# Loads of K, Q and V for two groups at a time, over one shared block of ones

## The chip, the cores and the metric

The kernel runs on one core of one Trainium2 chip. The time is the device time of the program in microseconds (us), taken from several runs; a profiled run gives the span and the trace, which begin a little later and end a little earlier than the timed run (before: 127.74 us timed, 126.0 us span). Ratios are the mean time of one kernel's fast runs over that of the other's fast runs of the same rounds, with a 95% interval; so they are not quite the ratio of the medians that stand beside them.

The engines are called PE (TensorE matmul), DVE (VectorE), ACT (ScalarE), POOL (GpSimd) and SP (SyncE).

## The reference

Linear attention on 8 x 12 heads, 512 positions, 64 dimensions, in fp32:

```python
Q_feat = np.maximum(0, Q) + 1
K_feat = np.maximum(0, K) + 1
KV = np.einsum('bhkd,bhkv->bhdv', K_feat, V)
K_sum = np.sum(K_feat, axis=2)
numerator = np.einsum('bhqd,bhdv->bhqv', Q_feat, KV)
denominator = np.einsum('bhqd,bhd->bhq', Q_feat, K_sum)
return numerator / (denominator[:, :, :, None] + 1e-10)
```

Q, K, V and the output are 12.58 MB each: 37.75 MB to read and 12.58 MB to write, with little arithmetic per byte.

## The kernel before

The work is cut into 12 groups of 8 heads. Each group needs K and Q on 128 partitions, and V as four blocks: block b holds V on partitions 32b to 32b+31 and zeros elsewhere; a fifth block holds ones in four columns, from which the matmul gets the sum of K. POOL issues the loads, which cast fp32 to bf16 (K of group 0 alone comes through SP, in fp32); it also issues most stores. Three V buffers, each with its own zeros and its own block of ones, go round. The code is cut, and the comments are added.

```python
NV = 3
v_blk = [const.tile([P, 5, 2, C2, D], BF16, name=f"v_blk{i}") for i in range(NV)]
...
def load_k(g):      # one DMA: 1.05 MB read, half of it written
    ...
def load_v(g):
    for b in range(4):
        nc.gpsimd.dma_start(
            out=v_blk[g % NV][32 * b : 32 * b + 32, b],
            in_=v_dram[32 * b : 32 * b + 32, 2 * g : 2 * g + 2],
        )
...
# the start: K and Q of groups 0 and 1 are issued, then
nc.vector.memset(flat[0][:, 0:part], 0.0)       # first clear, DVE's part; ACT has the rest
...
load_v(0)
nc.vector.memset(flat[1][:, 0:part], 0.0)       # second clear
...
make_identity(nc, identity)
for t in kva_diag:
    nc.gpsimd.memset(t, 0.0)
load_v(1)
load_k(2)
k_features(0)
q_features(0)
nc.vector.memset(flat[2][:, 0:part], 0.0)       # third clear
...
load_v(2)
load_q(2)
for g in range(NG - 1):
    if g:
        k_features(g); q_features(g); transposes(g - 1)
    if g >= 2:
        output(g - 2)
    keys_values(g)
    if g + AHEAD < NG:                          # AHEAD = 3
        load_k(g + AHEAD); load_v(g + AHEAD); load_q(g + AHEAD)
    if g >= LAG:
        store(g - LAG)
```

## Time and profile before

| | before |
|---|---|
| time, median (range) | 127.88 us (127.55 to 127.98) |
| span of the profiled run | 126.0 us |
| PE, DVE, ACT, POOL busy | 55%, 53%, 37%, 42% of the span |
| DMA, each of the 38 middle slices | 90% or more |
| transfers issued | 86 |

The row to read first is the DMA row: no engine that computes is busy much more than half of the time, and the DMA engines never rest. The prediction below shows these lines and works with them. The count of packets: 1376 small ones are the completions of 86 transfers on 16 engines.

```profile
DMA packets 14186, 32.13 MB, mean 255 GB/s; under 512 B 1376, under 2 KB 1376, under 8 KB 14176
```

### The profile page before, as it was taken

Reading aid. Unit: us, or ns where it says so; the run is one execution under the profiler, and the core shown is the slowest. Engines: PE = TensorE matmul, PEld = TensorE weight load, DVE = VectorE, ACT = ScalarE, POOL = GpSimd, SP = SyncE. Lnnn points to the kernel's source line nnn. Section 1 sums busy time; section 2 is a strip of 40 time slices with the busy share of each in tenths; the row PEclk is TensorE's granted clock in tenths of the full one; section 3 lists DMA queues with packets and bytes.
Section 4 is the critical chain, followed back from the end, with each engine's and each line's share of the span. In section 5 each row is a group of like instructions: output and inputs, shape, how many; then the busy total and the mean of one; then the engine's idle time right before and its main releaser. Section 6 shows DMA issues by size and latency. Waiting matters only on the chain.

```text
span 126.0 us, 2374 instructions
## 1 busy us (share of the span) xinstructions
PE 69.4 (55%) x960; PEld 51.1 (41%) x960; DVE 66.3 (53%) x155; ACT 47.1 (37%) x76; POOL 53.4 (42%) x91
## 2 busy tenths in 40 slices
PE   0000099719859089682971980890693496966100
PEld 0000087507647067462750660670562365744100
DVE  4898802077193582938607605723921944769400
ACT  7950007930645505554073054036019009290000
POOL 6695785616346156452372274263353341200000
PEclk9999999995999976999599589679869959996555
DMA  3999999999999999999999999999999999999993
GB/s 82 337 208 213 204 208 208 212 212 208 211 206 213 207 208 213 206 298 293 200 252 336 198 213 370 213 209 360 228 208 321 267 206 284 425 410 418 413 403 121
DMA packets 14186, 32.13 MB, mean 255 GB/s; under 512 B 1376, under 2 KB 1376, under 8 KB 14176
## 3 DMA queue, kind: packets, MB, share of 16 engines
q0 software_dynamic: 12816, 28.84, 98.8%
q1 hardware_dynamic: 1360, 3.15, 6.7%
q8 instruction: 7, 0.11, 0.3%
q14 instruction: 3, 0.02, 0.0%
HBM read 37.75 MB, written 12.58 MB: 400 GB/s over the span
## 4 chain that ended last, share of the span: by engine, by line
DMA 67%; DVE 9%; PE 8%; POOL 6%; issue 4%; POOLq 0%
DMA k_raw<-in_K_dram 25%; DMA q_raw<-in_Q_dram 17%; DMA v_blk<-in_V_dram 16%; DMA out_dram<-o_sb 9%; DVE o_sb L184 7%; PE kva_ps L141 5%; POOL v_blk L93 4%; POOL q_raw L100 2%; PE qt_ps L160 2%; DVE recip L183 1%; PE o_ps L173 1%; DVE qf L116 1%; POOL k_raw L86 1%; POOL zero L195 0%; POOLq L100 0%
## 5 line engine op out<-in xcount | busy, mean ns | idle before, releaser
L141 PE MATMUL kva_ps<-v_blk,kf 128*64 128x320 bf16 x384 | 40.6, 385 | 15.8 <-DMA v_blk<-in_V_dram 15.8
L141 PEld LDWEIGHTS <-kf 128*64 128x64 bf16 x384 | 27.9, 143 | 24.8 <-DVE qf L116 15.8
L93 POOL DMA_DIRECT2D v_blk<-in_V_dram x48 | 26.3, 552 | 27.0 <-DMA k_raw<-in_K_dram 14.8
L173 PE MATMUL o_ps<-kva_diag,qt 128*64 128x130 bf16 x384 | 19.1, 234 | 32.0 <-DVE o_sb L184 31.3
L184 DVE TENSOR_TENSOR o_sb<-o_ps,recip 128x512 f32<-128x512 f32 x48 | 33.2, 691 | 1.6
L151 ACT CAST kva_diag<-kva_ps 64x256 bf16<-64x256 f32 x24 | 8.9, 372 | 65.2 <-PE kva_ps L141 64.9
L161 ACT COPY qt<-qt_ps 128x1024 bf16<-128x1024 bf16 x24 | 29.5, 1301 | 0.3
L173 PEld LDWEIGHTS <-qt 128*64 128x64 bf16 x384 | 12.7, 114 | 37.5 <-DVE o_sb L184 35.8
L116 DVE TENSOR_SCALAR qf<-q_raw 128x1024 bf16<-128x1024 bf16 x24 | 9.2, 424 | 32.9 <-DMA q_raw<-in_Q_dram 32.9
L116 DVE TENSOR_SCALAR kf<-k_raw 128x1024 bf16<-128x1024 bf16 (+1 forms) x24 | 10.9, 497 | 10.3 <-DMA k_raw<-in_K_dram 10.3
L107 POOL DMA_DIRECT2D out_dram<-o_sb x10 | 7.7, 774 | 16.1 <-DMA q_raw<-in_Q_dram 7.8
L160 PE MATMUL qt_ps<-identity,qf 128*128 128x128 bf16 x192 | 13.1, 223 | 0.0
L160 PEld LDWEIGHTS <-qf 128*128 128x128 bf16 x192 | 11.1, 99 | 3.4 <-issue 3.2
L183 DVE RECIPROCAL recip<-o_ps 128x8 f32<-128x8 f32 x48 | 9.5, 198 | 4.1 <-PE o_ps L173 4.1
L86 POOL DMA_DIRECT2D k_raw<-in_K_dram x11 | 7.8, 713 | 8.4 <-DMA out_dram<-o_sb 3.7
L100 POOL DMA_DIRECT2D q_raw<-in_Q_dram x12 | 8.8, 730 | 4.4 <-DMA v_blk<-in_V_dram 2.5
L152 ACT CAST kva_diag<-kva_ps 64x4 bf16<-64x4 f32 x24 | 4.0, 168 | 0.0
L206 DVE MEMSET v_blk<- 128x2925 f32 x1 | 2.5, 2496 | 0.7 <-DVE ones L202 0.7
L224 DVE MEMSET v_blk<- 128x2925 f32 x1 | 2.5, 2496 | 0.6 <-issue 0.6
L212 DVE MEMSET v_blk<- 128x2925 f32 x1 | 2.5, 2496 | 0.6 <-issue 0.6
L219 POOL MEMSET kva_diag<- 128x520 bf16 x3 | 2.0, 720 | 0.0
L207 ACT COPY v_blk<-zero 128x2195 f32<-128x2195 f32 x1 | 2.0, 2020 | 0.0
(15 smaller groups left out, 7.9 us busy)
## 6 DMA issues: line engine op xcount, KB each, us to landing
out_dram<-o_sb POOLq DMA_DIRECT2D x10, 1024.0 KB, 12.1
q_raw<-in_Q_dram POOLq DMA_DIRECT2D x12, 512.0 KB, 11.1
v_blk<-in_V_dram POOLq DMA_DIRECT2D x48, 128.0 KB, 9.5
k_raw<-in_K_dram POOLq DMA_DIRECT2D x11, 512.0 KB, 12.0
out_dram<-o_sb SPq DMA_DIRECT2D x4, 512.0 KB, 7.6
k_raw<-in_K_dram SPq DMA_DIRECT2D x1, 1024.0 KB, 5.0
```

What stands on the lines that cost most here:

```text
L86: (nc.sync if g == 0 else nc.gpsimd).dma_start(out=k_raw, in_=k_dram[:, g * 2 : g * 2 + 2])
L93: nc.gpsimd.dma_start(out=v_blk[g % NV][32 * b : 32 * b + 32, b], in_=v_dram[32 * b : 32 * b + 32, 2 * g : 2 * g + 2],)
L100: nc.gpsimd.dma_start(out=q_raw, in_=q_dram[:, g * 2 : g * 2 + 2])
L107: nc.gpsimd.dma_start(out=o_to, in_=o_sb)
L116: nc.vector.tensor_scalar(out=dst, in0=src, scalar1=1.0, scalar2=1.0, op0=ALU.add, op1=ALU.max)
L141: nc.tensor.matmul(kva_ps[64 * n : 64 * n + 64], lhsT=kf[:, c, n, :], rhs=vb[:, :, n, c, :], start=(c == 0), stop=(c == C2 - 1),)
L151: nc.scalar.copy(out=kva[ps, :, n, 0:D], in_=kva_ps[ps, 0:4, :])
L160: nc.tensor.transpose(qt_ps[:, c, :], qf[:, half * C + c, :, :], identity)
L161: nc.scalar.copy(out=qt[:, :, :, half], in_=qt_ps)
L173: nc.tensor.matmul(ops[c // 4][64 * j : 64 * j + 64, c // 2 % 2, (c % 2) * W : (c % 2) * W + W], lhsT=qt[:, c, 32 * b : 32 * b + 32, :], r ...
L183: nc.vector.reciprocal(out=recip, in_=cells[:, :, :, :, D:D1])
L184: nc.vector.tensor_tensor(out=o_sb[:, h:NP:2, 4 * i : 4 * i + 4].rearrange("p n (b c) d -> p b c n d", b=2), in0=cells[:, :, :, :, 0:D], i ...
```

## The change

The intent is to have fewer and larger transfers: in the middle of the run K and Q of two groups come with one DMA each and V of two groups with four, and the loads stay two pairs ahead. Two V buffers, each for a pair of groups, are laid into one tile of nine blocks, 0 to 3 and 5 to 8, and share the ones in block 4; `own(g)` picks a group's half of its pair's buffer. The first two groups and the last two are still loaded one at a time. The core of the diff, cut, with one comment added:

```diff
-    v_blk = [const.tile([P, 5, 2, C2, D], BF16, name=f"v_blk{i}") for i in range(NV)]
+    v_all = const.tile([P, 9, 4, C2, D], BF16, name="v_all")
+    v_blk = [v_all[:, 5 * i : 5 * i + 4] for i in range(2)]
...
+    def own(g):
+        return slice(g % 2 * 2, g % 2 * 2 + 2)
...
+    def load(s):
+        pair = (2 * s, 2 * s + 1)
+        for groups in ((pair,) if s < NG // 2 - 1 else ((pair[0],), (pair[1],))):
+            load_k(s, groups)
+            load_v(s, groups)
+            load_q(s, groups)
...
+    def clear(blocks, ms, parts):       # DVE zeroes blocks up to parts, ACT the rest
...
-        nc.vector.memset(flat[0][:, 0:part], 0.0)
...
-        load_v(0)
-        nc.vector.memset(flat[1][:, 0:part], 0.0)
...
+        clear((0, 5), own(0), 3)
+        mark(own(0))
+        load_v(0, (0,))
+        clear((0, 5), own(1), 3)
+        mark(own(1))
         make_identity(nc, identity)
         for t in kva_diag:
             nc.gpsimd.memset(t, 0.0)
-        load_v(1)
-        load_k(2)
+        load_v(0, (1,))
+        load_k(1, (2, 3))
         k_features(0)
         q_features(0)
...
+        clear((5, 9), slice(0, 4), 7)
+        load_v(1, (2, 3))
+        load_q(1, (2, 3))
...
-            if g + AHEAD < NG:
-                load_k(g + AHEAD)
-                load_v(g + AHEAD)
-                load_q(g + AHEAD)
+            if g % 2 and g // 2 + 2 < NG // 2:
+                load(g // 2 + 2)
```

More of the change, by code (lines that the diff above doesn't have):

```diff
@@ L13 @@
 BANK = 512
-IN_BUFS = 4
+IN_BUFS = 2
 OUT_BUFS = 6
 LAG = 3
-AHEAD = 3
 @with_exitstack
@@ L73 @@
     kva_diag = [const.tile([P, 4, 2, D1], BF16, name=f"kva_diag{i}") for i in range(NV)]
+    k_bufs = {}
+    q_bufs = {}
     k_in = {}
@@ L80, with load_k, load_v, load_q @@
     outs = {}
-    def load_k(g):
-        k_raw = (head_pool if g == 0 else in_pool).tile(
-            [P, 2, C2, D], FP32 if g == 0 else BF16, name="k_raw"
-        )
-        (nc.sync if g == 0 else nc.gpsimd).dma_start(
-            out=k_raw, in_=k_dram[:, g * 2 : g * 2 + 2]
-        )
-        k_in[g] = k_raw
-    def load_v(g):
+    def own(g):
+        return slice(g % 2 * 2, g % 2 * 2 + 2)
+    def load_k(s, groups):
+        if groups == (0,):
+            k_raw = head_pool.tile([P, 2, C2, D], FP32, name="k_first")
+            nc.sync.dma_start(out=k_raw, in_=k_dram[:, 0:2])
+            k_in[0] = k_raw
+            return
+        if s not in k_bufs:
+            k_bufs[s] = in_pool.tile([P, 4, C2, D], BF16, name="k_raw")
+        ms = slice(groups[0] % 2 * 2, groups[-1] % 2 * 2 + 2)
+        nc.gpsimd.dma_start(
+            out=k_bufs[s][:, ms], in_=k_dram[:, 2 * groups[0] : 2 * groups[-1] + 2]
+        )
+        for g in groups:
+            k_in[g] = k_bufs[s][:, own(g)]
+    def load_v(s, groups):
+        ms = slice(groups[0] % 2 * 2, groups[-1] % 2 * 2 + 2)
         for b in range(4):
             nc.gpsimd.dma_start(
-                out=v_blk[g % NV][32 * b : 32 * b + 32, b],
-                in_=v_dram[32 * b : 32 * b + 32, 2 * g : 2 * g + 2],
-            )
-    def load_q(g):
-        q_raw = in_pool.tile([P, 2, C2, D], BF16, name="q_raw")
-        nc.gpsimd.dma_start(out=q_raw, in_=q_dram[:, g * 2 : g * 2 + 2])
-        q_in[g] = q_raw
+                out=v_blk[s % 2][32 * b : 32 * b + 32, b, ms],
+                in_=v_dram[32 * b : 32 * b + 32, 2 * groups[0] : 2 * groups[-1] + 2],
+            )
+    def load_q(s, groups):
+        if s not in q_bufs:
+            q_bufs[s] = in_pool.tile([P, 4, C2, D], BF16, name="q_raw")
+        ms = slice(groups[0] % 2 * 2, groups[-1] % 2 * 2 + 2)
+        nc.gpsimd.dma_start(
+            out=q_bufs[s][:, ms], in_=q_dram[:, 2 * groups[0] : 2 * groups[-1] + 2]
+        )
+        for g in groups:
+            q_in[g] = q_bufs[s][:, own(g)]
+    def load(s):
[4 more added lines that the diff above has]
+            load_q(s, groups)
     def store(g):
@@ L110, in store @@
             nc.sync.dma_start(out=o_to[:, h:NP:2], in_=o_sb[:, h:NP:2])
-    def edge(i):
-        return v_blk[i][:, 4, :, :, 0:4].rearrange("p n c j -> p (n c) j")
     def feature(dst, src):
@@ L136, in keys_values @@
         kf = kfs.pop(g)
-        vb = v_blk[g % NV]
+        sb = g // 2 % 2
+        vb = v_all[:, 4 * sb : 4 * sb + 5, own(g)]
         kva_ps = psum_kva.tile([P, 5, D], FP32, name="kva_ps")
@@ L150, in keys_values @@
             ps = slice(64 * n, 64 * n + 64)
-            nc.scalar.copy(out=kva[ps, :, n, 0:D], in_=kva_ps[ps, 0:4, :])
-            nc.scalar.copy(out=kva[ps, :, n, D], in_=kva_ps[ps, 4, 0:4])
+            nc.scalar.copy(out=kva[ps, :, n, 0:D], in_=kva_ps[ps, sb : sb + 4, :])
+            nc.scalar.copy(out=kva[ps, :, n, D], in_=kva_ps[ps, 4 - 4 * sb, 0:4])
     def transposes(g):
@@ L192, in output, with mark @@
         outs[g] = o_sb
+    def clear(blocks, ms, parts):
+        for eng, bs in zip((nc.vector, nc.scalar), (slice(blocks[0], parts), slice(parts, blocks[1]))):
+            t = v_all[:, bs, ms].rearrange("p b m c d -> p b (m c d)").bitcast(FP32)
+            if eng is nc.vector:
+                eng.memset(t, 0.0)
+            else:
+                eng.copy(out=t, in_=zero[:, :, None].to_broadcast([P, t.shape[1], t.shape[2]]))
+    def mark(ms):
+        e = v_all[:, 4, ms, :, 0:4].rearrange("p m c j -> p (m c) j")
+        nc.vector.tensor_copy(out=e, in_=ones[:, None, :].to_broadcast([P, e.shape[1], 4]))
     with tc.manual_schedule():
         nc.gpsimd.memset(zero, 0.0)
-        load_k(0)
-        load_q(0)
-        load_k(1)
-        load_q(1)
+        for g in range(2):
+            load_k(0, (g,))
+            load_q(0, (g,))
         nc.vector.memset(ones, 0.0)
@@ L202 @@
             nc.vector.memset(ones[32 * b : 32 * b + 32, b : b + 1], 1.0)
-        flat = [t.rearrange("p b n c d -> p (b n c d)").bitcast(FP32) for t in v_blk]
-        width = flat[0].shape[1]
-        part = width * 4 // 7
-        nc.vector.memset(flat[0][:, 0:part], 0.0)
-        nc.scalar.copy(
-            out=flat[0][:, part:width], in_=zero.to_broadcast([P, width - part])
-        )
-        nc.vector.tensor_copy(out=edge(0), in_=ones[:, None, :].to_broadcast([P, 2 * C2, 4]))
-        load_v(0)
-        nc.vector.memset(flat[1][:, 0:part], 0.0)
-        nc.scalar.copy(
-            out=flat[1][:, part:width], in_=zero.to_broadcast([P, width - part])
-        )
-        nc.vector.tensor_copy(out=edge(1), in_=ones[:, None, :].to_broadcast([P, 2 * C2, 4]))
+        clear((0, 5), own(0), 3)
[3 more added lines that the diff above has]
+        mark(own(1))
         make_identity(nc, identity)
@@ L219 @@
             nc.gpsimd.memset(t, 0.0)
-        load_v(1)
-        load_k(2)
+        load_v(0, (1,))
+        load_k(1, (2, 3))
         k_features(0)
         q_features(0)
-        nc.vector.memset(flat[2][:, 0:part], 0.0)
-        nc.scalar.copy(
-            out=flat[2][:, part:width], in_=zero.to_broadcast([P, width - part])
-        )
-        nc.vector.tensor_copy(out=edge(2), in_=ones[:, None, :].to_broadcast([P, 2 * C2, 4]))
-        load_v(2)
-        load_q(2)
+        clear((5, 9), slice(0, 4), 7)
+        load_v(1, (2, 3))
+        load_q(1, (2, 3))
         for g in range(NG - 1):
```

## The prediction

> **What bounds the kernel now.** I read the page's DMA rows first, then the chain of waits, then the busy table by stretch, then the timelines of the first 16 us and of one steady period.
>
> ```profile
> DMA  3999999999999999999999999999999999999993
> GB/s 82 337 208 213 204 208 208 212 212 208 211 206 213 207 208 213 206 298 293 200 252 336 198 213 370 213 209 360 228 208 321 267 206 284 425 410 418 413 403 121
> ...
> HBM read 37.75 MB, written 12.58 MB: 400 GB/s over the span
> ...
> DMA 67%; DVE 9%; PE 8%; POOL 6%; issue 4%; POOLq 0%
> ```
>
> The DMA engines are 90% busy or more in every slice between the first and the last, while PE is busy 55%, DVE 53%, POOL 42% and ACT 37% of the span. The GB/s row counts what is written: a load that casts fp32 to bf16 reads twice what it writes, so 208 to 213 there is 416 to 426 of reading, and the stores of the last slices move 403 to 425. Both kinds of traffic therefore run at about 419 GB/s of HBM bytes. All bytes are 37.75 + 12.58 = 50.33 MB; at 419 that is 120.1 us of the 126.0 us span. The rest is the start, the end, and small change. So: any moment in which the DMA queues are empty is added to the time, and faster engines gain nothing.
>
> The busy table by stretch (columns: stretch, its length, busy us of PE, PEld, DVE, ACT, POOL, granted clock, DMA share, GB/s) shows that they are empty only at the two ends:
>
> ```profile
> 0.00:2.00 2.00, 0.00 (x0) 0.00 (x0) 0.33 (x6) 1.26 (x1) 0.99 (x6) 1.00 0.10 18
> ...
> 10.00:15.00 5.00, 0.00 (x0) 0.00 (x0) 4.44 (x8) 0.00 (x0) 2.82 (x6) 1.00 1.12 209
> 15.00:20.00 5.00, 4.22 (x44) 3.40 (x45) 0.16 (x1) 0.44 (x3) 3.75 (x7) 1.00 1.11 207
> ...
> 124.00:126.00 2.00, 0.00 (x0) 0.00 (x0) 0.00 (x0) 0.00 (x0) 0.00 (x0) 0.50 0.06 25
> ```
>
> A steady period of the POOL timeline, whose transfers all go through one queue, gives the durations:
>
> ```profile
> 80.12 0.70 POOL L86 DMA_DIRECT2D k_raw<-in_K_dram  x1 [1.78 <-DMA out_dram<-o_sb]
> 82.57 2.18 POOL L93 DMA_DIRECT2D v_blk<-in_V_dram  x4 [1.76 <-DMA k_raw<-in_K_dram]
> 85.70 0.72 POOL L100 DMA_DIRECT2D q_raw<-in_Q_dram  x1 [0.95 <-DMA v_blk<-in_V_dram]
> 87.65 0.79 POOL L107 DMA_DIRECT2D out_dram<-o_sb  x1 [1.23 <-DMA q_raw<-in_Q_dram]
> 90.16 0.70 POOL L86 DMA_DIRECT2D k_raw<-in_K_dram  x1 [1.72 <-DVE recip L183]
> ```
>
> POOL waits before each issue for the landing of an earlier transfer of the same kind: in the built order each waits for the semaphore that the eighth transfer before it used (DMASW0 to 7 go round), so at most eight are in flight. The releases are thus landing times: store to K 2.45 us, K to Q 5.08 (four V and one Q), Q to store 2.51. A MB costs 2.5 us whatever its kind, and POOL's waits here cost nothing: about 10 us of transfers lie ahead in the queue.
>
> **What the Trainium skill says.** The Trainium skill, "DMA: Bandwidth & Descriptors", section "Bandwidth", advises to batch to 1 MiB and more for 75% of peak; that would speak for the change, whose K and Q loads double from 1 to 2 MB read and V pieces from 256 to 512 KB. The trace does not bear it out for a queue that stays full: with the small pieces it moves 419 GB/s already, against the 435 which the same section gives as the fabric's ceiling. The section "Anatomy of one DMA — SWDGE (gpsimd) path" puts about 2.0 us of fixed setup and completion on each transfer, most of it the wait for the last byte's confirmation, and says that DMA engines do not wait on semaphores, the issuing sequencer does. Back to back this overlaps, as the trace shows; where an issue must wait for a landing with nothing else queued it is paid. The section "Why a DMA increments its semaphore by 16 and not by 1" has each of 16 engines end a transfer with a small semaphore write. The page agrees: 1376 packets are under 512 B, and 10+12+48+11+4+1 = 86 issues times 16 is 1376.
>
> **The change part by part.**
>
> *Fewer, larger transfers.* K goes from 12 to 8 issues, Q from 12 to 8, V from 48 to 32; stores stay at 14. That is 86 to 62, or 24 x 16 = 384 small packets less. Bytes are the same. What one completion costs: over three periods V and Q together took 4.96, 5.02 and 5.08 us between releases (the last is shown above), mean 5.02; two K-sized transfers take 2 x 2.42 (2.39 and 2.45 seen). The 0.18 left is for three more completions: 0.06 each. 24 x 0.06 = 1.4 us at most; I take 0.8, since a V piece also differs in writing 32 partitions only. POOL saves some 24 issues of 0.54 to 0.73 us, off the path.
>
> *Depth of prefetch.* Two groups per slot, two slots. V for the next pair waits for the second group of the old pair. By hand, with 5 us for each pair transfer and 2.5 per store: after the V of a pair has landed, Q, K, V, Q, the next K and two to four stores (25 to 35 us) lie before the V that reuses its slot; Q's landing (5 us) and two compute iterations of about 6.5 us put that issue at about 18 us. The queue stays fed. At the tail POOL issues six stores after the last load instead of five; the last Q comes 2.5 us earlier and the sum of bytes is as before. Nothing lost, nothing won.
>
> *The first clears.* Here I see the cost. The timeline of before's start:
>
> ```profile
> 5.06 2.50 DVE L212 MEMSET v_blk<- 128x2925 f32 x1 [0.55 <-issue]
> ...
> 9.40 1.36 POOL L93 DMA_DIRECT2D v_blk<-in_V_dram  x2
> 11.17 0.54 POOL L93 DMA_DIRECT2D v_blk<-in_V_dram  x1 [0.41 <-issue]
> ...
> 13.44 0.75 POOL L93 DMA_DIRECT2D v_blk<-in_V_dram  x1 [1.74 <-DMA q_raw<-in_Q_dram]
> ...
> 14.18 0.72 POOL L86 DMA_DIRECT2D k_raw<-in_K_dram  x1
> ...
> 15.78 3.66 PE L141 MATMUL kva_ps<-v_blk,kf 128*64 128x320 bf16 x32 [15.78 <-DMA v_blk<-in_V_dram]
> ```
>
> The second clear runs at 5.06, so V of group 1 is issued from 9.40 and follows V of group 0 without a gap. In the changed kernel groups 0 and 1 share one tile, and the built order has a wait that was not there:
>
> ```
> DVE  L222 Memset v_all 128x3x1024 [waits DMASW5_49,DMASW4_49]
> POOL L107 DMACopy v_all<-in_V_dram 32x2x1024 [waits DVE_49]
> ```
>
> Those two semaphores, each at its first count, are the second and third V transfers of group 0. No byte overlaps: the clear is for group 1's part of blocks 0 to 2. But the stretch from its first to its last address takes in group 0's part of blocks 1 and 2, which is exactly what is waited for (blocks 0 and 3 are not). So the second clear begins when the third V piece has landed, and POOL, which runs in order, can issue V of group 1 and all that follows only after it. By then the queue has drained.
>
> Sizes: Q of group 1 landed at 13.16 (the POOL row at 13.44 and the chain), V pieces of 0.63 us follow: the third at 13.16 + 3 x 0.63 = 15.05, the fourth at 15.7 (PE starts at 15.78). The clear has 3072 columns: 2.50 x 3072/2925 = 2.62 us, to 17.7. From landing to landing the skill's fixed cost is about 2.0; the fourth piece still moves 0.63 us meanwhile. Empty queue: 2.0 - 0.63 + 2.62 + 0.1 to 0.6 for semaphores and issue = 4.1 to 4.6, taken as 4.4.
>
> *After it.* DVE then has the mark of ones, the features of K (2.48) and Q (0.74) of group 0 and a clear of 4096 columns (3.50), about 7.4 with gaps: to about 25.2, when V of groups 2 and 3 may go. V of group 1 and the K pair (2.5 + 5) feed the queue from about 19.3 to 26.8; first data of V about 1.5 us after 25.2. Just covered; I add 0.3.
>
> Sum: +4.4 +0.3 -0.8 = +3.9; 127.88 + 3.9 = 131.8 us.
>
> **Rivals.** (1) The wait is hidden and only the packets count: 127.88 - 0.8 = 127.1, at best 126.5. For it: landings of other transfers hide POOL's waits all through the middle. Against it: at 15 us nothing else can be queued, since POOL stands at the wait. (2) The middle starves as well, because V of a pair waits for two groups' matmuls, which are slowed to 4.01 us each where the clock is granted at 0.83 or less: one bubble of 1 us per pair in four pairs, 136. Against it: the 7 us and more of slack above. (3) Larger transfers move at a better rate: 425 in place of 419 GB/s would take 1.7 us off, to 130.1. For it: 425 stands in one slice of stores; against it: stores of 1 MB and V pieces of 128 KB written run alike.
>
> **Range and chances.** The bubble can be 3.5 to 5.2, the second gap 0 to 1, the saving 0 to 1.8: 130.2 to 133.2 should hold it 8 times in 10. Slower by over 2% begins at 130.44, so it is likely: 0.87. Within 2% (a short bubble with a large saving): 0.12. Faster by over 2% would need 125.3, less than the bytes allow with any gap: 0.01.
>
> **What would show it.** In the busy table the stretch 15 to 19 us should have a DMA share far under 0.5, where before it was 1.11. In the timeline the second DVE clear should start at about 15.1 instead of 5.06, released by a V landing, and V of group 1 be issued at about 17.8. DMA packets under 512 B should be 62 x 16 = 992. From 27 us to the end the DMA row should be full again and the spacing of releases 5 us per pair transfer. I am wrong if the second clear starts before 10 us, if the DMA row has gaps past 30 us, or if the released spacing is shorter than 4.9 us per 2 MB by more than the completions explain.

## The result, and the profile after

The changed kernel took 135.63 us (median of four runs, 134.18 to 136.11) beside 127.90 for the kernel before: ratio 1.0591, interval 1.0503 to 1.0679. Executions over 1.5% slower than the fastest of the same kernel are left out of the means. It is slower, as forecast, but by 7.7 us and not by 3.9; 135.63 lies outside the range of 130.2 to 133.2.

The page of the changed kernel has these rows in place of those quoted of before:

```profile
DMA  4999509899999999999999999999999999999991
GB/s 110 312 211 210 95 0 132 137 200 211 210 210 214 209 210 212 212 212 208 211 240 407 298 189 209 209 229 405 313 208 209 210 227 393 422 419 411 402 389 57
DMA packets 13803, 32.12 MB, mean 239 GB/s; under 512 B 993, under 2 KB 993, under 8 KB 13793
```

A slice is 134.2/40 = 3.36 us. The sixth slice (16.8 to 20.1 us) moves nothing, and the two after it 132 and 137 GB/s where slices with loads alone write about 210. From the ninth on the row is as full as before, to the end. The packets under 512 B are 993: 62 completions of 16, and one more packet.

The busy table by stretch puts numbers on it (columns: stretch, its length, busy us of PE, PEld, DVE, ACT and POOL with counts, granted clock, DMA share, GB/s written). The kernel before had 207 GB/s from 15 to 20 us (the prediction shows that line), and then, followed by the changed kernel:

```profile
20.00:28.00 8.00, 4.72 (x80) 3.62 (x77) 2.86 (x8) 6.14 (x10) 4.04 (x7) 1.00 1.13 210
```

```profile
15.00:20.00 5.00, 0.96 (x5) 0.50 (x7) 4.40 (x6) 0.00 (x0) 1.49 (x2) 1.00 0.00 0
20.00:28.00 8.00, 6.58 (x79) 5.12 (x76) 4.89 (x6) 3.36 (x6) 5.35 (x10) 1.00 0.92 141
28.00:40.00 12.00, 1.55 (x32) 1.28 (x31) 0.76 (x2) 3.33 (x6) 3.69 (x6) 0.69 1.12 209
```

In a kernel that is bound by its transfers, a stretch that moves a share of the full rate loses the rest of its length. With 210 GB/s as full: 15 to 20 us loses 5.0 us, 20 to 28 us loses 8 x (1 - 141/210) = 2.6 us, and after 28 us nothing is lost. The sum of 7.6 us is close to the measured 7.7 (the execution that was profiled is one of the slower two of its four: its span is 8.2 us longer, so that some 0.6 us of it lie elsewhere). So there are two parts: an **empty queue** of 5 us, and a **slow refill** of 8 us which costs half as much again.

The chain of waits, in order of time, shows how the first part comes about (start, duration, what):

```profile
5.96 8.87 DMA v_all<-in_V_dram
14.83 0.03 issue
14.86 0.02 DVEq L222
14.88 0.72 issue
15.60 2.62 DVE v_all L222
```

The third V piece of group 0 was issued at 5.96 and landed at 14.83. DVE's second clear had waited for it, began 0.77 us later and took 2.62. The timeline of POOL and DVE goes on from there:

```profile
15.60 2.62 DVE L222 MEMSET v_all<- 128x3072 f32 x1 [10.94 <-DMA v_all<-in_V_dram]
...
18.51 2.77 POOL L107 DMA_DIRECT2D v_all<-in_V_dram  x4 [9.49 <-DVE v_all L228]
...
20.93 3.47 DVE L222 MEMSET v_all<- 128x4096 f32 x1 [0.80 <-issue]
21.28 0.77 POOL L98 DMA_DIRECT2D k_raw<-in_K_dram  x1
```

POOL stood for 9.49 us and issued V of group 1 at 18.51, where the kernel before did so from 9.40. The first packet of it started at 20.25, after 5.1 us without any (the last packet before ended at 15.14).

The second part was not foreseen. The packet records of the trace show what it consists of: a packet of a load (4 KB read, 2 KB written) takes 173 ns in the steady stretches. The first seven packets after the restart took 638 to 685 ns, those from 21 to 22 us 173 again; then, about 2 us after the restart, eleven packets that ran side by side took several times as long, and some went on to do so until 28 us. These are the durations in ns of packets that started from 22.29 to 22.6 us in the changed kernel and took over 400:

```
806 776 739 682 720 645 621 640 644 686 455
```

### The profile page after: what moved, and what is told of

The parts are those of the page before. It is cut to its first block, busy times and chain, and to the rows that moved or that the text cites. A ratio compares the mean times of both kernels' runs of the same rounds, so it can differ in the third digit from the quotient of the medians.

```text
span 134.2 us, 2337 instructions
## 1 busy us (share of the span) xinstructions
PE 65.7 (49%) x960; PEld 48.9 (36%) x960; DVE 65.6 (49%) x154; ACT 48.7 (36%) x76; POOL 39.6 (29%) x67
## 4 chain that ended last, share of the span: by engine, by line
DMA 45%; DVE 22%; PE 20%; issue 4%; POOL 3%; DVEq 0%; POOLq 0%
DMA q_raw<-in_Q_dram 31%; DMA v_all<-in_V_dram 14%; PE kva_ps L165 12%; DVE o_sb L208 10%; DVE v_all L222 6%; PE qt_ps L184 4%; PE o_ps L197 4%; POOL v_all L107 3%; DVE recip L207 2%; DVE qf L139 1%; DVE kf L139 1%; DVE ones L237 0%; DVE v_all L228 0%; DVE ones L235 0%; DVEq L222 0%
## 5 line engine op out<-in xcount | busy, mean ns | idle before, releaser
L165 PE MATMUL kva_ps<-v_all,kf 128*64 128x320 bf16 x384 | 36.5, 353 | 20.5 <-DVE kf L139 18.9
L197 PE MATMUL o_ps<-kva_diag,qt 128*64 128x130 bf16 x384 | 19.8, 239 | 39.1 <-DVE o_sb L208 38.6
L165 PEld LDWEIGHTS <-kf 128*64 128x64 bf16 x384 | 25.6, 132 | 27.9 <-DVE kf L139 19.4
L107 POOL DMA_DIRECT2D v_all<-in_V_dram x32 | 18.5, 583 | 38.6 <-PE kva_ps L165 14.2
L222 DVE MEMSET v_all<- 128x3072 f32 (+1 forms) x3 | 8.7, 2903 | 12.4 <-DMA v_all<-in_V_dram 10.9
L139 DVE TENSOR_SCALAR kf<-k_raw 128x1024 bf16<-128x1024 bf16 x22 | 8.2, 417 | 7.0 <-DMA k_raw<-in_K_dram 6.9
L98 POOL DMA_DIRECT2D k_raw<-in_K_dram x7 | 5.2, 744 | 19.5 <-DVE kf L139 10.1
L116 POOL DMA_DIRECT2D q_raw<-in_Q_dram x8 | 6.0, 755 | 6.3 <-DMA q_raw<-in_Q_dram 4.4
L224 ACT COPY v_all<-zero 128x2048 f32<-128x2048 f32 (+1 forms) x3 | 7.3, 2464 | 0.8 <-DVE v_all L228 0.8
L139 DVE TENSOR_SCALAR kf<-k_first 128x1024 bf16<-128x1024 f32 x2 | 1.3, 682 | 0.0
## 6 DMA issues: line engine op xcount, KB each, us to landing
q_raw<-in_Q_dram POOLq DMA_DIRECT2D x4, 1024.0 KB, 17.8
q_raw<-in_Q_dram POOLq DMA_DIRECT2D x4, 512.0 KB, 10.2
```

Source lines behind the costliest of these rows:

```text
L107: nc.gpsimd.dma_start(out=v_blk[s % 2][32 * b : 32 * b + 32, b, ms], in_=v_dram[32 * b : 32 * b + 32, 2 * groups[0] : 2 * groups[-1] + 2],)
L139: nc.vector.tensor_scalar(out=dst, in0=src, scalar1=1.0, scalar2=1.0, op0=ALU.add, op1=ALU.max)
L165: nc.tensor.matmul(kva_ps[64 * n : 64 * n + 64], lhsT=kf[:, c, n, :], rhs=vb[:, :, n, c, :], start=(c == 0), stop=(c == C2 - 1),)
L197: nc.tensor.matmul(ops[c // 4][64 * j : 64 * j + 64, c // 2 % 2, (c % 2) * W : (c % 2) * W + W], lhsT=qt[:, c, 32 * b : 32 * b + 32, :], r ...
L222: eng.memset(t, 0.0)
L224: eng.copy(out=t, in_=zero[:, :, None].to_broadcast([P, t.shape[1], t.shape[2]]))
```

## The experiments

All kernels gave correct results. The diffs are cut; where a run builds on another, only what it adds is shown. "Loss" in the table is the sum over the stretches 15 to 20 and 20 to 28 us of length x (1 - GB/s / 210), worked out from the busy table of each; "measured" is the median less that of the kernel before in the same set of runs.

| run | time us | ratio (interval) | GB/s 15-20, 20-28 | loss us | measured us |
|---|---|---|---|---|---|
| clears_first | 127.93 | 1.0006 (0.9957 to 1.0056) | 194, 211 | 0.3 | +0.3 |
| clears_first_5 | 127.92 | 1.0023 (0.9982 to 1.0065) | 195, 211 | 0.3 | +0.3 |
| singles | 127.97 | 0.9993 (0.9935 to 1.0052) | 204, 209 | 0.2 | +0.3 |
| before_wait | 134.56 | 1.0516 (1.0462 to 1.057) | 5, 169 | 6.4 | +6.9 |
| after_again | 135.20 | 1.0581 (1.0549 to 1.0613) | 3, 141 | 7.6 | +7.4 |
| third_early | 136.09 | 1.0634 (1.0558 to 1.0709) | 3, 135 | 7.8 | +8.4 |
| quiet_dve | 134.93 | 1.0559 (1.053 to 1.0587) | 3, 161 | 6.8 | +7.1 |
| k_second | 134.60 | 1.0551 (1.051 to 1.0593) | 5, 154 | 7.0 | +6.8 |
| k_ahead | 130.33 | 1.0206 (1.0139 to 1.0273) | 210, 146 | 2.4 | +2.5 |
| kq_ahead | 127.55 | 0.9986 (0.9943 to 1.0029) | 212, 210 | 0.0 | -0.1 |
| k_by_sp | 132.93 | 1.0403 (1.0361 to 1.0446) | 8, not comparable | 4.8 for 15-20 | +5.3 |
| stand_longer | 138.68 | 1.0861 (1.0791 to 1.093) | 0, 74 | 10.2 | +11.0 |

### Is it the wait?

**clears_first** moves one line of the changed kernel: V of group 0 is issued after both clears, so the second clear stands behind no landing.

```diff
         mark(own(0))
-        load_v(0, (0,))
         clear((0, 5), own(1), 3)
         mark(own(1))
+        load_v(0, (0,))
```

> The changed kernel with one line moved: V of group 0 is issued after both clears of the shared tile, so the second clear no longer stands behind two V landings. Theory 1 (the false wait makes the whole loss: 5.2 us of empty queue and the poor refill after it): the queue never empties, the DMA share stays over 1.05 from 4 us on, and 24 fewer completions leave 126.8 to 127.7, just under the kernel before. Theory 2 (pair loads themselves cost something later, by starved or uneven engines): the empty queue goes but 2 to 3 us of the loss stay, 129.5 to 131.

It took 127.93 us beside 127.67. The two stretches of its busy table are full again:

```profile
15.00:20.00 5.00, 4.27 (x41) 3.40 (x42) 0.88 (x3) 0.32 (x2) 3.75 (x6) 1.00 1.10 194
20.00:28.00 8.00, 4.45 (x75) 3.51 (x72) 0.76 (x2) 6.25 (x12) 2.36 (x4) 1.00 1.13 211
```

Theory 1 holds and theory 2 falls: pair loads, the shared ones and the larger slots all stayed, and with the wait the whole loss went. The time came out 0.2 us over the expected band, which counted on a saving by fewer completions; that is taken up below. The trace also shows which bytes the waits go by. The V piece for block 0, which lies before the first address of the second clear, was issued at 4.90 us; the next three were held for that clear until 8.15.

**before_wait** is the opposite: the kernel before, with the wait alone put in.

```diff
         load_v(0)
+        probe = const.tile([P, 4], BF16, name="probe")
+        nc.vector.tensor_copy(out=probe[64:96, :], in_=v_blk[0][64:96, 2, 0, 0, 0:4])
         nc.vector.memset(flat[1][:, 0:part], 0.0)
```

> The kernel before with nothing changed but one read of 32 x 4 elements of the third V piece of group 0 by DVE, ahead of its second clear: the same wait, without pairs. Theory 1 (the wait alone makes the loss): about 5.2 us empty near 15 to 20 us, slow refill, 24 more completions than the changed kernel: 135 to 137. Theory 2 (pairs cost some of it): 132.5 to 134.

It took 134.56 us, 0.44 under the band of theory 1 and 0.56 over that of theory 2. The empty stretch is the same (5 GB/s), the refill somewhat better (169 GB/s in place of 141). So the wait by itself makes 6.9 us of loss without any pair; the 0.5 to 0.8 us between this and the changed kernel lie in the refill, and whether the size of the K pair makes them was not settled.

**stand_longer** makes the second clear twice, so that POOL stands longer.

```diff
         clear((0, 5), own(1), 3)
+        clear((0, 5), own(1), 3)
```

> The changed kernel with the second clear of 3072 columns made twice, so that POOL stands 2.6 us longer on an empty queue. If the empty queue is the bound, all of it adds: 2.6 us over the changed kernel, 137.5 to 138.5. If part of the loss were hidden by slack later: less than 1.5 us more.

It took 138.68 us (137.87 to 139.78). The second of the two clears cost not 2.62 us but 3.3, since 0.7 us passed between them, and V of group 1 was issued at 21.86 where it was 18.75 in after_again. 3.1 us of standing made 3.5 us more (138.68 less 135.20, from two sets of runs): nothing of it is hidden. The refill did not grow with the stand. The queue was empty for 8.4 us (15.20 to 23.61), and the rates up to 33 us give a loss of 10.9 in all, so the refill cost 2.5 as in the changed kernel. It runs past 28 us here, and this is why the 10.2 of the table falls short of 11.0.

**after_again** is the changed kernel as it was, a control in the second set of runs.

> The changed kernel unaltered, on the chip of these runs, as a control: 134.2 to 136.5 as on record.

It took 135.20 us (134.81 to 135.56).

### Are the pairs worth anything?

**singles** has the shared tile and both clears first, but loads one group at a time and three ahead:

```diff
-            if g % 2 and g // 2 + 2 < NG // 2:
-                load(g // 2 + 2)
+            if g + 3 < NG:
+                load_k((g + 3) // 2, (g + 3,))
+                load_v((g + 3) // 2, (g + 3,))
+                load_q((g + 3) // 2, (g + 3,))
```

> The shared tile and block of ones of the changed kernel and both clears first, but loads of one group at a time, three ahead, as before. Against clears_first it shows what the pair loads alone do, against the kernel before what the layout alone does. If the layout costs nothing: 127.5 to 128.2. If 24 completions are worth 0.02 to 0.06 us each, clears_first is 0.5 to 1.4 us below this; if pairs do harm, it is above.

It took 127.97 us, clears_first in the same runs 127.93. **clears_first_5** measures the latter with five rounds:

> clears_first with five rounds, to tell whether the pairs with 24 fewer completions are worth anything against the kernel before: ratio 0.990 to 0.996 if a completion costs 0.02 to 0.06 us; 0.997 to 1.003 if its cost is hidden.

The ratio is 1.0023 with an interval from 0.9982 to 1.0065. That excludes a net saving of over 0.2%; neither the layout nor the pairs do anything that these runs can tell from nothing. The net figure contains a loss of about 0.3 us from 15 to 20 us (195 GB/s), where the K pair came 3.3 us after its issue, so by this estimate the pairs by themselves are worth 0.5 us at most. The packets of the kernel before give a better estimate than the releases did: four V pieces took 2.54 us (first packets from 20.06 to 22.60 us), one K or Q 2.49, so that each further transfer costs 0.02 us and 24 of them about 0.4. The expected gain of 0.8 was not there to be had.

### What makes the refill slow?

**third_early** moves the third clear (4096 columns, 20.9 to 24.4 us in the changed kernel) ahead of the second, into time in which DVE idles. The Trainium skill, "SBUF — State Buffer", section "SBUF: two separate sides", says that DVE in some modes locks GpSimd out of a shared port, so that descriptors can't be written; DVE was therefore the first suspect, although that page names copy, cast and tensor_scalar for it and not a memset.

```diff
         mark(own(0))
+        clear((5, 9), slice(0, 4), 7)
         load_v(0, (0,))
...
         q_features(0)
-        clear((5, 9), slice(0, 4), 7)
         load_v(1, (2, 3))
```

> The changed kernel with the false wait kept, but the third clear (4096 columns on DVE, 20.9 to 24.4 us) moved ahead of the second, into the time in which DVE idles. Theory A (that clear holds up the writing of DMA descriptors, so V of group 1 and the first K pair come slowly from 22 to 26 us): the empty stretch of about 5.2 us stays, the slow stretch goes, K pair lands about 2 us earlier, 133.0 to 134.0. Theory B (a queue that restarts from empty is slow for a few us whatever DVE does, or POOL's own issue rate limits it): 135 to 136 as the changed kernel.

136.09 us, 135 GB/s in the refill: the slow stretch stayed. Theory A falls.

**quiet_dve** also moves the features of groups 0 and 1 ahead of the waiting clear, so DVE does nothing in the refill.

```diff
         load_v(0, (0,))
+        for g in range(2):
+            k_features(g)
+            q_features(g)
         clear((0, 5), own(1), 3)
...
-        k_features(0)
-        q_features(0)
...
```

> third_early, and the features of K and Q of groups 0 and 1 also moved ahead of the waiting second clear, so DVE does nothing from about 18.3 us until K of group 2 has landed. Theory A2 (DVE's feature operations at 18.2 to 21.6 hold up POOL's issues of V and the descriptors of the K pair): the four V issues take 2.1 us in place of 2.8 to 3.1 and the refill costs 0.5 or less: 132.8 to 134. Theory B (the refill is slow whatever DVE does): 135 to 136.5.

134.93 us beside 135.20 for after_again, a difference within the spread of the runs, and beside 136.09 for third_early in another set. The four V issues took 2.13 us in place of 2.78, as the page would have it for tensor_scalar, and the refill ran at 161 GB/s in place of 141 (135 in third_early). That is a part of it at most: with DVE idle from 20 to 28 us, 1.9 us were still lost there, beside 2.6 and 2.9. PE's work on group 0 also came earlier in this run, so that the part is not DVE's for certain. Theory A2 falls as the main cause.

**k_second** issues one V piece after the stand, then the K pair, then the other three pieces.

```diff
-        load_v(0, (1,))
-        load_k(1, (2, 3))
+        load_v(0, (1,), (0,))
+        load_k(1, (2, 3))
+        load_v(0, (1,), (1, 2, 3))
```

> The changed kernel, but after the stand POOL issues one V piece, then the K pair, then the other three V pieces. The empty 5 us stay. Theory C (the refill is slow because four V pieces of 0.63 us each are issued every 0.7 us, so that engines run dry between them): the refill gets faster, 133.5 to 134.5. Theory D (the refill is slow for another reason, such as the big K pair itself): 135 to 136.5.

134.60 us beside 135.20: between the two expectations, just over theory C's, and the ranges of the two overlap. The slow packets now fell into the first V piece (at 20.5 us) and the beginning of the K pair (from 21.8 to 23.2 us) and the rate was full from 24 us. Small pieces following one another are not the cause by themselves either.

**k_ahead** (third_early, with the K pair issued before POOL comes to the waiting V) keeps the wait but puts 5 us of transfers into the queue.

```diff
         load_v(0, (0,))
+        load_k(1, (2, 3))
         clear((0, 5), own(1), 3)
...
         load_v(0, (1,))
-        load_k(1, (2, 3))
```

> third_early, and the K pair of groups 2 and 3 issued before POOL comes to the waiting V of group 1. The false wait stays, but 2 MB of reading (5 us) lie in the queue while POOL stands. Theory 1 (the loss is the empty queue and its refill): the stretch 15 to 20 us is full, V of group 1 comes at about 20 us, at most 0.5 us empty: 127.7 to 129. Theory 2 (the late V of group 1 or the late features cost by themselves through the chain of compute): 132 or more, with a full queue.

130.33 us, between the two theories, and the most telling run. The queue was never empty, and yet the refill was as slow as ever:

```profile
15.00:20.00 5.00, 0.74 (x3) 0.31 (x5) 4.26 (x6) 0.00 (x0) 1.35 (x3) 1.00 1.12 210
20.00:28.00 8.00, 8.00 (x83) 5.70 (x80) 2.65 (x8) 3.40 (x7) 4.98 (x8) 1.00 0.99 146
```

The queue was only short: POOL began to issue at 18.65, and by 20.6 the K pair had landed. The slow refill is thus not the price of idle engines starting up; it goes with transfers that POOL issues shortly before their turn.

**kq_ahead** puts the Q pair ahead of the stand too, so that 10 us of transfers lie in the queue.

```diff
         load_k(1, (2, 3))
+        load_q(1, (2, 3))
         clear((0, 5), own(1), 3)
...
         load_v(1, (2, 3))
-        load_q(1, (2, 3))
```

> k_ahead with the Q pair of groups 2 and 3 issued ahead of the stand as well, so about 10 us of transfers lie in the queue when POOL may go on at 18.5 us, instead of 5. k_ahead lost 2.5 us with a queue that was never empty, in a slow stretch from 20 to 28 us whose transfers were issued only 1.5 to 4.5 us before their data. Theory S (transfers issued shortly before their turn run slow; issued 5 us or more ahead they run at full rate): 127.4 to 128.4, no stretch under 200 GB/s. Theory L (the late V of group 1 holds up compute, and that costs the rest): 130 or more.

127.55 us beside 127.65, inside the band of theory S. POOL stood until the same moment as in k_ahead (18.50 and 18.65 us), and issued seven V pieces in one go as k_ahead its eight; DVE did the same features beside it:

```profile
18.50 4.68 POOL L107 DMA_DIRECT2D v_all<-in_V_dram  x7 [7.56 <-DVE v_all L228]
```

```profile
15.00:20.00 5.00, 0.97 (x5) 0.49 (x7) 4.42 (x6) 0.00 (x0) 1.50 (x2) 1.00 1.13 212
20.00:28.00 8.00, 5.05 (x45) 3.29 (x41) 2.98 (x9) 3.33 (x6) 4.66 (x8) 0.97 1.12 210
```

The seven V pieces were issued 5.9 to 7.3 us before their first packets (the first at 18.50 for 24.91), and every piece ran at full rate. The late V of group 1, which theory L feared for, cost nothing.

**k_by_sp** keeps the empty queue (third_early) but takes the K pair through SP's queue, in fp32, released by DVE together with V of group 1.

```diff
         load_v(0, (1,))
-        load_k(1, (2, 3))
+        k_sp = head_pool.tile([P, 4, C2, D], FP32, name="k_sp")
+        nc.vector.memset(k_sp[:, 0, 0, 0:2], 0.0)
+        nc.sync.dma_start(out=k_sp, in_=k_dram[:, 4:8])
```

> third_early (136.1), but the K pair after the stand comes through SP's queue in fp32, released by DVE when V of group 1 is. POOL's own first transfers after the stand then have other traffic beside them, and 2 MB of the refill are not issued by POOL. Theory P (the slow stretch belongs to transfers issued late by POOL): the K pair runs beside V at full total rate, the refill costs 0.5 us or less instead of 2.4: 133 to 134. Theory G (any restart of the engines is slow for some us, whoever issues): 135 to 136.5.

132.93 us, 3.2 under third_early and even a little under the band of theory P. Of the loss of 5.3, 4.2 are the time without a packet (15.42 to 19.63), so the restart cost about 1:

```profile
15.00:20.00 5.00, 0.64 (x3) 0.30 (x5) 4.16 (x6) 0.00 (x0) 1.25 (x3) 1.00 0.09 8
20.00:28.00 8.00, 5.81 (x47) 3.90 (x45) 1.78 (x6) 3.33 (x6) 4.95 (x8) 1.00 1.03 320
```

The 320 GB/s are not to be set beside 210, since SP's load writes fp32, as many bytes as it reads. POOL's transfers had SP's ahead of them and so a later turn: the first V piece, issued at 18.75, had its first packet at 23.19. SP's own first packets were slow too (up to 824 ns from 20 to 20.5 us), but by 21 us the engines ran at full rate. Theory G falls: a restart from empty is slow for little more than a us, not for eight.

What is shown: the refill costs 1.6 to 2.9 us where POOL feeds a queue that is empty or short, about 1 us where SP's transfer goes first (k_by_sp), and nothing where POOL's transfers have a longer lead (kq_ahead), the lead being the time from a transfer's issue to its first packet. How long a lead is enough can be read from the packets of all kept traces, matched in order to POOL's issues of loads before 31 us (roughly, where the engines drift apart). With a lead under 3 us, 12% of the packets took over 250 ns (36 transfers); with 3 to 3.6 us, 3%; with 3.6 to 5.5 us, 0.4%; beyond that, 0.1%. So these traces show a slope and no threshold. In the kernel before, transfers with 3.4 and 3.5 us of lead had no slow packet, while one with 4.0 us in k_ahead had 20 of 128.

What stays open: by what means a late issue makes packets slow. That descriptors come late would fit, since packets took up to 1.2 us with their engine counted as busy; but no run here looks at descriptors, and the lock on DVE's port explains a part at most.

## Why the prediction was wrong, step by step

- **DMA is the bound, and any empty moment adds to the time.** Right. The sums over the stretches give the measured loss to within half a us in nine of the eleven runs for which both stretches can be compared (to 0.6 and 0.8 in the other two; of the 0.8, stand_longer lost 0.7 after 28 us), and stand_longer shows that more standing adds in full.
- **POOL waits for the eighth transfer before.** Right: in the trace the eight semaphores of POOL's transfers go round. But that is not one "of the same kind", as the prediction's own lines show: K waits for a store, V for K, the store for Q; and beside the last of these lines (90.16) stands an operation of DVE, not a landing. Nothing rests on the slip. Nor can the 419 GB/s of HBM bytes be held against the 435: the section gives that ceiling for the ports of SBUF, where these loads write only 210.
- **The built order has a false wait, and POOL stands behind it.** Right. The second clear was released by a V landing, at 15.60 instead of 15.1; V of group 1 went out at 18.51 instead of 17.8. clears_first took the wait out and with it the loss; before_wait put it in alone.
- **The empty queue: 4.1 to 4.6, taken as 4.4.** Too small by 0.7; 5.1 us passed without a packet. From the third landing to the first new packet the trace has 0.77 us to the start of the clear, 2.62 for the clear, 0.29 to the issue and 1.74 to the packet, in all 5.42, of which the fourth piece covered 0.31. The transfer's part, 1.74 less 0.31, is the 2.0 less 0.63 that were expected; semaphores and issue came to 1.06 and not to 0.1 to 0.6. Most of it is the 0.72 that the chain calls "issue" before the clear. The kernel before had shown such a delay: its second clear stood 0.55 us on issue as well.
- **After it: "Just covered; I add 0.3".** This is the step that failed most. It took the full rate for granted as soon as V of group 1 and the K pair were issued, and looked only for a gap between them. There was no such gap, but 8 us at two thirds of the rate, 2.6 us in place of 0.3.
- **Saving by 24 fewer completions: 0.8.** Not there. clears_first_5 is 0.3 us over the kernel before, with an interval that excludes a saving of over 0.25 us. The 0.06 us for each that the working drew from three periods rests on a difference of 0.18 us between sums of landing times that themselves vary by 0.12; the packets give 0.02.
- **Depth of prefetch and the tail.** Right: from 28 us the rates are those of before, a pair transfer takes 5 us (first packets of Q and the next K at 35.25 and 40.20), and POOL's longer waits cost nothing.
- **The sum:** 5.0 + 2.6 - 0 = 7.6 against +4.4 + 0.3 - 0.8 = +3.9; measured 7.7. Of the signs named ahead, the share of the stretch 15 to 20 us (0.00), the release and the packets (993 for 992) came as said, and there was no gap past 30 us. Of the rivals, the first (the wait is hidden) fell with the profile. The second (the middle starves) and the third (larger transfers run better) fell with clears_first.

The mechanism of the wait and the direction were right; the slow refill was in no part of the prediction. Two terms of the sum were too small, and the saving was booked on a difference too small to carry it.

## What to carry to other kernels

Where several buffers become parts of one tile, look in the built order for waits that no shared byte explains: a strided clear was held here for transfers that only lie between its first and its last address (which transfers waited, in the changed kernel and in clears_first, fits this; no run varied it further), and POOL, which issues in order, held back everything behind it. In a kernel bound by transfers, the time for which the queue is empty is lost, and a slow refill comes on top (here 1.6 to 2.9 us, and no more after 8.4 us of empty queue than after 5.1). A stand costs nothing if the queue still holds enough when the issuing engine goes on: 6.4 us of transfers were enough in kq_ahead, and 1.4 us were too few in k_ahead. Before a gain is expected from larger transfers, check that the queue is not full already: here it was, and fewer transfers were worth nothing.

## What the Trainium skill lacked or had wrong

- "DMA: Bandwidth & Descriptors", section "Bandwidth": its rule to batch to 1 MiB or more does not say whether other transfers are queued. In a full queue V pieces of 256 KB read, with K and Q of 1 MB, did as well as pieces of 512 KB with 2 MB: ratio 1.0023 (0.9982 to 1.0065) for clears_first_5 against the kernel before.
- The same page, section "Anatomy of one DMA — SWDGE (gpsimd) path": by its formula the first V piece (0.26 MB read) on an empty queue would land 2.6 us after its issue, an estimate. It took 2.8 us in quiet_dve, which is near, but 3.3 us in the changed kernel, where DVE's features run beside it.
- No page found says how far ahead of its turn a transfer from GpSimd has to be issued. With 1.4 to 5.1 us of lead the rate from 20 to 28 us was 146 GB/s written (k_ahead), with 5.9 and more 210 (kq_ahead), the packets of the former taking 400 to 1100 ns at times in place of 173.
- No page found gives the time that passes before a large DVE memset starts: 0.77 us after the landing here, and 0.80 on "issue" before the third clear, which waits for no landing.
- "SBUF — State Buffer", section "Who interferes with whom": it has tensor_scalar able to contend with GpSimd. That agrees: four V issues took 2.78 us beside the features and 2.13 without them. It does not account for the slow refill, which ran at 161 GB/s with DVE idle.
